# Zero products issued beside the weighted sums in the first grouped-query unit and the first neighbourhood head of each layer's attention

## The chip, the cores and the metric

The kernel runs on one core of a Trainium2 chip. The metric is the device time of one execution in microseconds (us). The time before is the median of three runs. A separate profiled execution gives the rows that are read below.

## What is computed

Two layers of a transformer block work on 1024 latent tokens and 256 context tokens of width 1024. Each layer has a token-mixing part with four parallel groups, and an MLP. Two of the four groups matter here: grouped-query attention (four query heads, two key heads of 64) and neighbourhood attention (four heads of 64, a window of 8 x 16 on a grid of 64 columns, with a learned bias). Cut to that:

```python
def attend(qi, kk, vv):
    s = jnp.einsum('bqkgd,bskd->bkgqs', qi, kk).astype(jnp.float32)
    p = jax.nn.softmax(s, axis=-1).astype(vv.dtype)
    return jnp.einsum('bkgqs,bskd->bqkgd', p, vv)
...
z = modulate(rms_norm(x, g_pre_mix), sh1, sc1) @ w_in
oa, oac = gqa_mixer(z, zc, ...)
ob, obc = s5_mixer(z, zc, ...)
on, onc = na_mixer(z, zc, ...)
od = fourier_mixer(z, w_fnet, b_fnet)
y = jnp.concatenate([oa, ob, on, od], axis=-1) @ w_out
x = x + g1 * rms_norm(y, g_post_mix)
h = modulate(rms_norm(x, g_pre_mlp), sh2, sc2)
x = x + g2 * rms_norm(sq_relu_mlp(h, w_mlp1, w_mlp2), g_post_mlp)
```

The context tokens go through the same weights in the first layer alone, where they are queries too.

## The kernel before

Tokens are cut into ten tiles of 128 (eight latent, two of context). A layer runs the input projection, then a phase that the function `attention` lays out, then the output projection and the MLP. Most products on TensorE are split into three (lines 161 to 163: high by high, low by high, high by low part), so that four-byte precision is kept.

The attention phase is a list of units that run one after the other. Six grouped-query units come first in layer 0 (two key heads, each with two blocks of four query tiles and one block of two context tiles) and four in layer 1, then four neighbourhood heads. A unit has two halves:

- The preparation, `gqa_prep` or `na_prep`. It transposes queries and keys (line 522), makes the scores once to find the largest of each row (products at lines 586 and 593, VectorE's maxima at 588 and 595; in a neighbourhood head 720, 729 and 747 with VectorE at 722, 730 and others), and writes the negative maximum as one more row of the queries. For a grouped-query unit the transposes of `ql` (line 522) carry it there. For a neighbourhood head it goes through a transpose (line 752), a copy to `nmt` and a DMA into the queries.
- The main half, `gqa_main` or `na_main`. For each key tile it makes scores already less the maximum (lines 653 or 778, two products that add up), ScalarE takes the exponential (654 or 782), and the weighted sums follow one key tile later (`pv`, line 622): products of 65 columns, of which the last is the sum of the weights. At the end VectorE divides (`divide`), and `finish` transposes the result (line 683).

The sums of a unit stand in one tile of two PSUM banks, `po`, of which there is one buffer. `sums` (line 613) opens both banks with a product of zeros: one row of 128 zeros by one row of as many zeros as the sums have columns (260 for a unit of four tiles, 130 for the context unit, 325 for a head with context queries). A unit's sums thus wait until the division of the unit before has read `po`. Scores have their own two buffers (`s1`), and the preparation has others.

The main half of a unit is woven with the preparation of the next one, and with the scan of the S5 group (lines 1291 to 1324) and the Fourier group (161 to 163 on `uh`, `csh`). The order of the instructions on each engine is set when the kernel is built: a scheduler walks through the program with its own estimate of durations and takes, among the instructions that are ready, the one of the best priority. On the chip every engine then takes its instructions strictly in that order. TensorE is one such queue, so a product that waits holds all that stand behind it.

Of the kernel before, what the change touches and what calls it, by code (L numbers as in the profile page):

```python
# [19 lines left out]
NT = 10  # L20
# [12 lines left out]
class K:  # L33
# [571 lines left out]
        self.transposes(q2, lambda i: ql[:, i // n, i % n, :], 2 * n)  # L605
        yield

    def sums(self, n):


        po = self.ps2(tag="pO")
        for b in range(2):
            self.nc.tensor.matmul(po[:, b * 512:b * 512 + n * 65], self.zero[:, :128], self.zero[:, :n * 65],
                                  start=True, stop=False)
        return po

    def pv(self, queue, vf, kt, po, parts, end=()):


        def whole():  # L620
            for (b, c), e in parts:
                self.nc.tensor.matmul(po[:, b * 512 + c * 65:b * 512 + c * 65 + 65], e, vf[:, kt, :],  # L622
                                      start=False, stop=(b, c) in end)
        queue.append((2, whole))
# [12 lines left out]
    def gqa_main(self, st, u, o):  # L637
        nc = self.nc
        q1, q2 = u["q"]
        k1, k2 = u["k"]  # L640
        vf = st["zg"][:, :, 384 + 65 * u["j"]:449 + 65 * u["j"]]
        w = u["n"] * 128
        kts = range(8, NT) if u["b"] == 2 else range(NT)
        po = self.sums(u["n"])
        queue = []
        for kt in kts:
            ks = slice(kt * 128, (kt + 1) * 128)
            e = st["pg"].tile([128, 1024], F32, tag="e", bufs=4, name="e")[:, :2 * w]
            for h in range(2):
                ps = self.ps1(tag="s1")[:, :w]  # L650
                hs = slice(h * w, (h + 1) * w)
                for kk, qq in ((k1, q1), (k2, q2)):
                    nc.tensor.matmul(ps, kk[:, ks], qq[:, hs], start=kk is k1, stop=kk is k2)
                nc.scalar.activation(e[:, hs], ps, AF.Exp)  # L654
            yield
            self.due(queue)
            self.pv(queue, vf, kt, po, [((h, t), e[:, h * w + t * 128:h * w + (t + 1) * 128])
                                        for h in range(2) for t in range(u["n"])],
                    [(h, u["n"] - 1) for h in range(2)] if kt == NT - 1 else ())
            yield  # L660
        self.due(queue, True)
        n = u["n"]
        on = st["fp"].tile([128, 4, 2, 64], F32, tag="on", bufs=2, name="on")
        self.divide(st, po, on[:, :n].rearrange("p t h d -> p h t d"), n)
        st["fin"] = self.finish(lambda t: on[:, t].rearrange("p h d -> p (h d)"), n, o, u["j"], u["t0"])
        yield
# [91 lines left out]
    def na_main(self, st, u, o):  # L758
        nc, s = self.nc, st["n"][u["h"] % 2]
        h, nq, bt = u["h"], u["nq"], s["bt"]  # L760
        k1, k2, q1, q2 = (s[n] for n in ("k1", "k2", "q1", "q2"))
        po = self.sums(nq // 256)
        queue = []
        for i, kt in enumerate((8, 0, 1, 2, 3, 4, 5, 6, 7, 9)):
            ks = slice(kt * 128, (kt + 1) * 128)
            ra, rb = (0, 16) if kt >= 8 else self.NA_ROWS_OF[kt]
            pieces = [(x * 64, y * 64) for x, y in ((ra, min(rb, 8)), (max(ra, 8), rb)) if x < y]

            r0 = ra - ra % 2
            e = st["pg"].tile([128, 1024], F32, tag="e", bufs=4, name="e")[:, :(rb - r0) * 64]  # L770
            if r0 < ra:
                nc.gpsimd.memset(e[:, 0:64], 0.0)
            f0 = (ra - 2 * kt + 6) if kt < 4 else 12 + (ra - 2 * kt + 3)
            for x, y in pieces:
                ps = self.ps1(tag="s1")[:, :y - x]
                ee = e[:, x - r0 * 64:y - r0 * 64]
                for kk, qq in ((k1, q1), (k2, q2)):
                    nc.tensor.matmul(ps, kk[:, ks], qq[:, x:y], start=kk is k1, stop=kk is k2)
                if kt < 8:
                    self.tt(ee, ps, bt[:, f0 + x // 64 - ra:f0 + y // 64 - ra, :].rearrange("p a b -> p (a b)"), OP.add)  # L780
                    ps = ee
                nc.scalar.activation(ee, ps, AF.Exp)
            yield
            self.due(queue)
            self.pv(queue, s["vf"], kt, po, [((t % 2, t // 2), e[:, t * 128 - r0 * 64:(t + 1) * 128 - r0 * 64])
                                             for t in range(r0 // 2, rb // 2)], [(0, 3), (1, 3)] if i == 9 else ())
            yield
            if i == 0 and nq > NLAT:

                ps = self.ps1(tag="s1").rearrange("p (b n) -> p b n", b=2)  # L790
                for c in range(2):
                    ks = slice(1024 + c * 128, 1152 + c * 128)
                    nc.tensor.matmul(ps[:, c, :], k1[:, ks], q1[:, 1024:1280], start=True, stop=False)
                    nc.tensor.matmul(ps[:, c, :], k2[:, ks], q2[:, 1024:1280], start=False, stop=True)
                e = st["pg"].tile([128, 1024], F32, tag="e", bufs=4, name="ec")[:, :512]
                nc.scalar.activation(e.rearrange("p (b n) -> p b n", b=2), ps, AF.Exp)
                yield
                self.due(queue)
                for c in range(2):
                    self.pv(queue, s["vf"], 8 + c, po, [((t, 4), e[:, c * 256 + t * 128:c * 256 + (t + 1) * 128])  # L800
                                                        for t in range(2)])
                yield
        self.due(queue, True)
        if h % 2 == 0:
            st["on"] = st["fp"].tile([128, NT, 2, 64], F32, tag="onn", bufs=1, name="onn")
        on = st["on"]
        n = nq // 256
        self.divide(st, po, on[:, :2 * n, h % 2].rearrange("p (c b) d -> p b c d", b=2), n)
        st["fin"] = iter(())
        if h % 2:  # L810
            st["fin"] = self.finish(lambda t: on[:, t].rearrange("p h d -> p (h d)"), 2 * n, o, 4 + h // 2, 0)
        yield
# [1036 lines left out]
```

## Time and profile before

| | us |
|---|---|
| median of three runs | 3044.02 |
| lowest and highest of the three | 3028.48 and 3049.46 |
| the profiled execution, its own time | 3037.68 |
| its span, first to last instruction | 3035.5 |
| TensorE busy in it | 2916.6 |

TensorE (PE) is busy in 96% of the span. PEld is its loading of weights, which lies beside its products. DVE is VectorE, ACT ScalarE, POOL GpSimd. [...] Times in rows are us from the start of the span, and "idle before <-releaser" is how long the engine stood still ahead of the instruction and whose result ended that.

### The profile page before, as it was taken

What the parts mean: (1) busy time and instruction counts of PE and PEld (TensorE: products, weight loads), DVE (VectorE), ACT (ScalarE), POOL (GpSimd) and SP (SyncE); (2) the same over time, 40 slices, a digit from 0 to 9 for tenths busy, and PEclk for the clock granted to TensorE, in tenths of its full rate; (3) what the DMA queues carried; (4) which work ended last, traced back from release to release, by engine and by line L of the source; (5) the groups of instructions that cost most, each with busy time, mean ns of one, the idle gap of its engine ahead of it and who ended that gap; (6) DMA issues with size and microseconds to landing.
All of it is one profiled execution on the core that took longest, in us unless ns stands there. A gap on an engine that the chain in (4) does not pass through costs nothing. (4 is left out here: it accounts for less than half of the span.)

```text
span 3035.5 us, 41960 instructions
## 1 busy us (share of the span) xinstructions
PE 2916.6 (96%) x16492; PEld 2538.7 (84%) x16492; DVE 1635.7 (54%) x2245; ACT 1078.5 (36%) x1850; POOL 912.6 (30%) x859
## 2 busy tenths in 40 slices
PE   6999999999999999999999899999999999999998
PEld 3798898888888889898988788888877888888887
DVE  3565565664776544754554676565754343344334
ACT  3544555453422222422222345365643212211222
POOL 1474223125421112611212555123234111111113
PEclk8999899999999999999999999999999999999999
DMA  7533425332543322432332534425343111111113
GB/s 267 187 115 116 93 79 140 113 138 97 184 141 132 129 84 84 160 118 98 111 117 99 169 110 133 92 73 154 106 160 111 56 42 56 42 56 42 56 42 111
DMA packets 233494, 334.87 MB, mean 110 GB/s; under 512 B 43120, under 2 KB 179408, under 8 KB 233296
## 3 DMA queue, kind: packets, MB, share of 16 engines
q1 hardware_dynamic: 233296, 332.18, 35.0%
q8 instruction: 130, 2.13, 0.3%
q14 instruction: 68, 0.56, 0.1%
HBM read 278.53 MB, written 53.54 MB: 109 GB/s over the span
## 5 line engine op out<-in xcount | busy, mean ns | idle before, releaser
L161 PE MATMUL ps<-mh,wh 128*128 128x320 f32 (+1 forms) x1536 | 518.9, 338 | 9.3 <-DVE y L155 6.1
L149 ACT ACTIVATE wh<-raw 128x1024 fp32r<-128x1024 f32 x234 | 243.1, 1057 | 795.3 <-PE ps L163 551.1
L163 PE MATMUL ps<-mh,wl 128*128 128x320 f32 (+1 forms) x1536 | 517.1, 337 | 0.9 <-DVE wl L152 0.9
L162 PE MATMUL ps<-ml,wh 128*128 128x320 f32 (+1 forms) x1536 | 517.6, 337 | 0.0
L161 PE MATMUL ps<-wh,hidh 128*128 128x512 f32 x1152 | 451.6, 392 | 2.1 <-DVE y L155 2.0
L163 PE MATMUL ps<-wh,hidl 128*128 128x512 f32 x1152 | 447.8, 390 | 2.7 <-POOL hidl L152 2.7
L162 PE MATMUL ps<-wl,hidh 128*128 128x512 f32 x1152 | 449.2, 390 | 0.0
L155 DVE TENSOR_TENSOR y<-ps,y 128x1024 f32<-128x1024 f32 (+1 forms) x253 | 306.6, 1218 | 260.5 <-PE ps L163 260.4
L152 POOL TENSOR_TENSOR hidl<-r,hidh 128x640 fp32r<-128x640 f32 (+1 forms) x128 | 190.5, 1489 | 679.6 <-DVE r L155 654.9
L152 DVE TENSOR_TENSOR wl<-raw,wh 128x1024 fp32r<-128x1024 f32 x188 | 286.4, 1533 | 176.0 <-ACT wh L149 167.5
L161 PEld LDWEIGHTS ps<-mh,wh 128*128 128x128 f32 x1536 | 290.0, 189 | 34.8 <-issue 7.3
L163 PEld LDWEIGHTS ps<-mh,wl 128*128 128x128 f32 x1536 | 289.9, 189 | 21.5 <-DVE wl L152 1.5
L162 PEld LDWEIGHTS ps<-ml,wh 128*128 128x128 f32 x1536 | 289.9, 189 | 20.8
L161 PEld LDWEIGHTS ps<-wh,hidh 128*128 128x128 f32 x1152 | 216.7, 188 | 53.2 <-issue 5.8
L152 POOL TENSOR_TENSOR wl<-raw,wh 128x1024 fp32r<-128x1024 f32 x48 | 117.4, 2447 | 467.3 <-ACT wh L149 467.1
L163 PEld LDWEIGHTS ps<-wh,hidl 128*128 128x128 f32 x1152 | 216.5, 188 | 48.9 <-POOL hidl L152 3.5
L162 PEld LDWEIGHTS ps<-wl,hidh 128*128 128x128 f32 x1152 | 216.7, 188 | 43.3
L155 DVE TENSOR_TENSOR r<-r 128x640 f32<-128x640 f32 (+1 forms) x128 | 98.9, 773 | 241.4 <-ACT hidh L1515 241.3
L1513 ACT ACTIVATE r<-ps 128x640 f32<-128x640 f32 (+1 forms) x128 | 82.3, 645 | 366.2 <-PE ps L163 360.4
L622 PEld LDWEIGHTS ps<-zg,e 128*128 128x128 f32 x1312 | 181.8, 195 | 15.0 <-ACT e L654 0.8
L622 PE MATMUL ps<-zg,e 128*128 128x65 f32 x1312 | 175.6, 270 | 0.4 <-ACT e L654 0.4
L294 DVE SCALAR_TENSOR_TENSOR acc<-raw,cst,acc 128x1024 f32<-128x1024 f32 x70 | 99.3, 1443 | 136.0 <-DMA raw<-in_w_ada_dram 136.0
(434 smaller groups left out, 5448.0 us busy)
## 6 DMA issues: line engine op xcount, KB each, us to landing
raw<-in_w_mlp_dram SPq DMA_DIRECT2D x192, 512.0 KB
raw<-in_w_ada_dram SPq DMA_DIRECT2D x96, 512.0 KB
raw<-in_w_in_dram SPq DMA_DIRECT2D x28, 512.0 KB
x<-x SPq DMA_DIRECT2D x26, 512.0 KB
x<-h SPq DMA_DIRECT2D x18, 512.0 KB
x<-in_x_dram SPq DMA_DIRECT2D x16, 512.0 KB
raw<-in_w_out_dram SPq DMA_DIRECT2D x16, 512.0 KB
bq<-in_na_bq_dram SPq DMA_DIRECT2D x8, 800.0 KB
```

The costliest lines, as they stand in the source:

```text
L149: self.nc.scalar.activation(out, in_, AF.Copy, scale=scale)
L152: (eng or self.nc.vector).tensor_tensor(out=out, in0=a, in1=b, op=OP.subtract)
L155: (eng or self.nc.vector).tensor_tensor(out=out, in0=a, in1=b, op=op)
L161: self.nc.tensor.matmul(ps, ah, bh, start=start and i == 0, stop=False)
L162: self.nc.tensor.matmul(ps, ah, bl, start=False, stop=False)
L163: self.nc.tensor.matmul(ps, al, bh, start=False, stop=stop and i == n - 1)
L294: nc.vector.scalar_tensor_tensor(acc[c], x, col, acc[c], op0=OP.mult, op1=OP.add)
L622: self.nc.tensor.matmul(po[:, b * 512 + c * 65:b * 512 + c * 65 + 65], e, vf[:, kt, :], start=False, stop=(b, c) in end)
L1513: nc.scalar.activation(r.rearrange("p (b n) -> p b n", b=nb), ps[:, :nb, :w], AF.Relu)
```

## The change

Four stages are marked as idle: the first grouped-query unit of each layer, and neighbourhood head 0 of each layer. In a marked stage three things differ.

First, bank 0 of `po` is opened 512 wide instead of 260 (or 325). Second, after the weighted sums of each key tile eight products of zeros are issued, 128 columns wide, into columns 384 to 512 of that bank, which the sums do not use. Each has one row of 128 zeros as its weights and one row of 128 zeros as its data, in bf16. They are issued at a priority lowered by 60, which gives the scheduler leave to place them later than their place in the program. Third, the flag that closes bank 0 moves from the last weighted sum to one more product of zeros, 512 wide, which stands ahead of the division.

There are ten key tiles in each marked stage, so 80 products of zeros in each, 320 in all, with four closing ones and four wider opening ones. No other instruction is added or taken away. Apart from these, the order of instructions differs only in the attention phases of the two layers.

```diff
-    def sums(self, n):
+    def sums(self, n, idle=False):
         po = self.ps2(tag="pO")
         for b in range(2):
-            self.nc.tensor.matmul(po[:, b * 512:b * 512 + n * 65], self.zero[:, :128], self.zero[:, :n * 65],
-                                  start=True, stop=False)
+            w = 512 if idle and not b else n * 65
+            self.nc.tensor.matmul(po[:, b * 512:b * 512 + w], self.zero[:, :128], self.zero[:, :w], start=True, stop=False)
         return po
+
+    def idle(self, po, n, end=False):
+        if end:
+            self.nc.tensor.matmul(po[:, 0:512], self.zero[:, :128], self.zero[:, :512], start=False, stop=True)
+            return
+        with self.tc.high_priority(offset=-60):
+            for _ in range(n):
+                self.nc.tensor.matmul(po[:, 384:512], self.zero[:, :128], self.zero[:, :128], start=False, stop=False)
...
+        idle = u is st["units"][0]
+        po = self.sums(u["n"], idle)
...
-                    [(h, u["n"] - 1) for h in range(2)] if kt == NT - 1 else ())
+                    [(h, u["n"] - 1) for h in range(idle, 2)] if kt == NT - 1 else ())
+            if idle:
+                self.idle(po, 8)
             yield
         self.due(queue, True)
+        if idle:
+            self.idle(po, 0, True)
...
-        po = self.sums(nq // 256)
+        po = self.sums(nq // 256, h == 0)
...
+            if h == 0:
+                self.idle(po, 8)
             yield
...
         self.due(queue, True)
+        if h == 0:
+            self.idle(po, 0, True)
```

In the changed kernel `sums` stands at line 614, the closing product at 621, the products of zeros at 625, the weighted sums at 632, the scores at 664 (before: 653) and 793 (778), the head's score maxima at 744 (729), the transposes of the result at 698 (683). Lines below 613 keep their numbers.

Where the products of zeros stand is the scheduler's choice. On TensorE, at the start of unit 0 of layer 0, the kernel before has these rows (`g0k` and `g0q` are the keys and queries of unit 0, `g1q` the queries of the next unit, `ql` the queries that carry the maximum):

```order
L653 MATMUL ps<-g0q_2780,g0k_2776 128x512 x2
L586 MATMUL ps<-g0k_2776,g0q_2780 128x512
L613 LDWEIGHTS zero
L613 MATMUL ps<-zero 128x260
...
L586 MATMUL ps<-g0k_2776,g0q_2780 128x512 x5
L593 MATMUL ps<-g0k_2776,g0q_2780 128x256 x8
L522 MATMUL ps<-identr,ql 128x128 x8
```

In the changed kernel the same place reads as follows, with the pair of L625 rows sixteen times:

```order
L664 MATMUL ps<-g0q_2780,g0k_2776 128x512 x2
L586 MATMUL ps<-g0k_2776,g0q_2780 128x512
L614 LDWEIGHTS zero
L614 MATMUL ps<-zero 128x512
...
L614 MATMUL ps<-zero 128x260
L625 LDWEIGHTS zero
L625 MATMUL ps<-zero 128x128
...
L586 MATMUL ps<-g0k_2776,g0q_2780 128x512 x5
L593 MATMUL ps<-g0k_2776,g0q_2780 128x256 x8
L522 MATMUL ps<-identr,ql 128x128 x8
```

Sixteen products of zeros, those of two key tiles, stand right behind the opening of the sums, ahead of the five remaining products whose maxima VectorE waits for, and none stands behind those.

On TensorE at the end of unit 0 of layer 0, the kernel before has these rows (`g1q` are the queries of unit 1, `khl` the keys of the next key head, `on` the result of unit 0):

```order
L622 MATMUL ps<-zg,e 128x65 x4
L653 MATMUL ps<-g1q_3290,g0k_2776 128x512
L653 MATMUL ps<-g1q_3291,g0k_2777 128x512
...
L522 MATMUL ps<-identr,ql 128x128 x4
L522 MATMUL ps<-identr,khl 128x128 x4
L653 MATMUL ps<-g1q_3290,g0k_2776 128x512
L653 MATMUL ps<-g1q_3291,g0k_2777 128x512
L613 LDWEIGHTS zero
L613 MATMUL ps<-zero 128x260
```

The changed kernel has these, with the pair of L625 rows two times at the first place and six times at the second:

```order
L625 LDWEIGHTS zero
L625 MATMUL ps<-zero 128x128
...
L664 MATMUL ps<-g1q_3290,g0k_2776 128x512
L664 MATMUL ps<-g1q_3291,g0k_2777 128x512
L625 LDWEIGHTS zero
L625 MATMUL ps<-zero 128x128
...
L632 MATMUL ps<-zg,e 128x65 x6
L522 MATMUL ps<-identr,khl 128x128 x4
L632 MATMUL ps<-zg,e 128x65 x5
L522 MATMUL ps<-identr,khl 128x128 x2
L632 MATMUL ps<-zg,e 128x65 x4
L621 MATMUL ps<-zero 128x512
```

Weighted sums of unit 0 and products of zeros now stand between the first scores of unit 1 and the transposes of the keys, where before the scores of unit 1 ended the stage.

On TensorE in neighbourhood head 0 of layer 0 the kernel before has these rows (`n0` is head 0, `n1` head 1 in preparation, `nvf` the values):

```order
L729 MATMUL ps<-n1k_5228,n1q_5232 128x512
L778 MATMUL ps<-n0q_4891,n0k_4887 128x512
L778 MATMUL ps<-n0q_4892,n0k_4888 128x512
L778 MATMUL ps<-n0q_4891,n0k_4887 128x256
L778 MATMUL ps<-n0q_4892,n0k_4888 128x256
L622 MATMUL ps<-nvf_4893,e 128x65 x5
L729 MATMUL ps<-n1k_5228,n1q_5232 128x512 x2
L778 MATMUL ps<-n0q_4891,n0k_4887 128x192
```

The changed kernel has these, where the pairs of L625 rows stand three, two, eight and three times, in this order:

```order
L793 MATMUL ps<-n0q_4972,n0k_4968 128x512
L793 MATMUL ps<-n0q_4973,n0k_4969 128x512
L625 LDWEIGHTS zero
L625 MATMUL ps<-zero 128x128
...
L744 MATMUL ps<-n1k_5309,n1q_5313 128x512
L625 MATMUL ps<-zero 128x128
...
L632 MATMUL ps<-nvf_4974,e 128x65 x3
L625 MATMUL ps<-zero 128x128
...
L632 MATMUL ps<-nvf_4974,e 128x65 x2
L793 MATMUL ps<-n0q_4972,n0k_4968 128x256
L793 MATMUL ps<-n0q_4973,n0k_4969 128x256
L632 MATMUL ps<-nvf_4974,e 128x65 x2
L625 MATMUL ps<-zero 128x128
...
```

Here the products of zeros are scattered ahead of and behind the products of L744 whose maxima VectorE takes.

## Rows read from the trace of the kernel before

**Rows 1.** The page: span, busy time, granted clock in 40 slices

```profile
span 3035.5 us, 41960 instructions
...
PE 2916.6 (96%) x16492; PEld 2538.7 (84%) x16492; DVE 1635.7 (54%) x2245; ACT 1078.5 (36%) x1850; POOL 912.6 (30%) x859
...
PEclk8999899999999999999999999999999999999999
```

**Rows 2.** Busy time of each engine in stretches of the attention phases

```profile
core 0: us, PE busy (x) PEld busy (x) DVE busy (x) ACT busy (x) POOL busy (x), PEclk, DMA share, GB/s
...
315.07:328.73 13.66, 12.12 (x43) 9.72 (x44) 6.47 (x12) 5.89 (x9) 2.16 (x3) 0.50 0.81 153
328.73:362.86 34.13, 34.13 (x251) 31.71 (x250) 23.62 (x48) 21.71 (x43) 11.33 (x19) 1.00 0.33 85
...
366.27:376.51 10.24, 10.24 (x48) 8.99 (x47) 0.82 (x1) 6.14 (x13) 0.59 (x2) 0.50 0.02 8
...
516.46:536.94 20.48, 20.01 (x82) 18.74 (x83) 12.99 (x31) 9.13 (x22) 8.93 (x11) 0.50 0.28 91
...
550.59:554.01 3.42, 3.42 (x16) 3.11 (x15) 2.39 (x7) 1.07 (x2) 0.00 (x0) 0.50 1.02 220
...
1932.99:1939.82 6.83, 5.73 (x19) 4.03 (x18) 3.18 (x5) 5.44 (x9) 1.94 (x2) 0.50 1.22 137
1939.82:1977.37 37.55, 37.18 (x277) 34.91 (x277) 26.71 (x50) 22.23 (x44) 15.21 (x22) 1.00 0.43 116
2096.83:2110.48 13.65, 9.56 (x38) 8.35 (x38) 7.17 (x17) 2.57 (x6) 0.24 (x2) 0.50 0.83 222
2110.48:2137.00 26.52, 26.22 (x216) 24.62 (x215) 20.64 (x46) 17.87 (x38) 11.45 (x17) 1.00 0.41 131
```

**Rows 3.** All zero products of line 613: ns of one (min/median/max), forms

```profile
L613 PEld LDWEIGHTS <-zero x36: 90/93/112, 308.8 to 2196.7; 1*128 1x128 bf16 x36
L613 PE MATMUL ps<-zero x36: 215/279/418, 308.8 to 2196.8; 1*128 1x260 bf16 x24, 1*128 1x325 bf16 x8, 1*128 1x130 bf16 x4
```

**Rows 4.** Timeline of PE: a 130-column pair of zero products; start, us

```profile
495.47 0.28 PE L613 MATMUL ps<-zero 1*128 1x130 bf16 x2
```

**Rows 5.** Timeline of PE, start of unit 0 of layer 0

```profile
308.22 0.39 PE L653 MATMUL ps<-g0q,g0k 128*128 128x512 f32 x1
308.45 0.40 PE L586 MATMUL ps<-g0k,g0q 128*128 128x512 f32 x1
308.78 0.39 PE L613 MATMUL ps<-zero 1*128 1x260 bf16 x2
309.10 1.03 PE L586 MATMUL ps<-g0k,g0q 128*128 128x512 f32 x2
```

**Rows 6.** Timeline of DVE in the same place

```profile
308.89 4.01 DVE L588 TENSOR_REDUCE nm<-ps 128x1 f32<-128x512 f32 x6 [0.35 <-PE ps L586]
312.81 2.66 DVE L595 TENSOR_REDUCE nm<-ps 128x2 f32<-128x512 f32 x4
```

**Rows 7.** Timeline of PE, start of head 0 of layer 1

```profile
2099.84 0.61 PE L613 MATMUL ps<-zero 1*128 1x260 bf16 x2 [4.07 <-DVE on L155]
2100.38 0.27 PE L752 MATMUL ps<-identr,nmr 128*16 128x128 f32 x1
...
2107.41 1.19 PE L778 MATMUL ps<-n0q,n0k 128*128 128x512 f32 x2 [1.08 <-DMA n0q<-nmt]
```

**Rows 8.** Timeline of PE in head 0 of layer 0

```profile
515.23 0.50 PE L729 MATMUL ps<-n1k,n1q 128*128 128x512 f32 x1 [0.78 <-DVE mx L730]
516.58 0.80 PE L729 MATMUL ps<-n1k,n1q 128*128 128x512 f32 x1 [0.84 <-DVE mx L730]
```

**Rows 9.** Timeline of PE, end of unit 0 of layer 0

```profile
365.86 0.89 PE L653 MATMUL ps<-g1q,g0k 128*128 128x512 f32 x2 [1.48 <-ACT e L654]
366.68 0.61 PE L613 MATMUL ps<-zero 1*128 1x260 bf16 x2
```

**Rows 10.** Timeline of PE, head 0 to head 1 of layer 0

```profile
549.55 0.39 PE L161 MATMUL ps<-uh,fwh 128*128 128x258 f32 x1 [2.27 <-DVE gl L152]
```

More of the change, by code (lines that the diff above doesn't have):

```diff
@@ L643, in gqa_main @@
         kts = range(8, NT) if u["b"] == 2 else range(NT)
-        po = self.sums(u["n"])
+        idle = u is st["units"][0]
+        po = self.sums(u["n"], idle)
         queue = []
@@ L785, in na_main @@
             self.pv(queue, s["vf"], kt, po, [((t % 2, t // 2), e[:, t * 128 - r0 * 64:(t + 1) * 128 - r0 * 64])
-                                             for t in range(r0 // 2, rb // 2)], [(0, 3), (1, 3)] if i == 9 else ())
+                                             for t in range(r0 // 2, rb // 2)], [(b, 3) for b in range(h == 0, 2)] if i == 9 else ())
+            if h == 0:
+                self.idle(po, 8)
             yield
```

## The prediction

> **What bounds the kernel now.** I read the page first. TensorE is busy for 2916.6 us of a span of 3035.5 us, and its granted clock is a little under full in a few slices only [rows 1]. So the kernel is bound by TensorE almost everywhere, and a change that gives TensorE more to do has to earn its time back somewhere. The place to look for that is the clock. [...] Three things are to be seen there. At the start of unit 0 of layer 0 the low stretch lasts 13.66 us, but TensorE is busy for only 12.12 of it and VectorE is what it waits for. At the end of that unit a low stretch of 10.24 us is filled with TensorE's work to the last: 48 products and nothing else that counts. In head 0 of layer 0 a low stretch lasts 20.48 us with 20.01 busy. Layer 1 has two more, 6.83 and 13.65 us, with gaps in them, and between head 0 and head 1 of layer 0 there is one of 3.42 us. Between these stretches TensorE is at 1.00 and full: 34.13 of 34.13 us in unit 0 of layer 0, 37.18 of 37.55 in that of layer 1, 26.22 of 26.52 in head 0 of layer 1 [rows 2]. A product of zeros that stands there delays all that follows.
>
> **What one product of zeros costs.** The kernel already has such products, of 260, 325 and 130 columns. Their weight load takes 0.09 us [rows 3]. The pair of 130 columns lasts 0.28 us, of which the last product is 0.215 (the shortest) [rows 3, 4]. So the two start 0.065 us apart, and I take that for 128 columns; the load lies under the product before. A pair of 260 columns lasts 0.39 us with 0.27 to 0.28 for one, so 0.12 apart [rows 3, 5]. At the low clock the pair lasts 0.61 us with 0.418 for the longest one, so 0.19 apart [rows 3, 9]; a product of 128 columns is then about 0.10. A change between two kinds of product costs a little too: the 512-wide products before the pair start 0.23 us apart, but the pair starts 0.33 after the last of them, and the next product 0.32 after the pair, where twice 0.12 would do [rows 5]. That is 0.10 in and 0.08 out. The products of zeros stand in 66 groups, and where a group stands between score products and weighted sums TensorE changes kind anyway. I take 0.10 a group; the ends are 0 and 0.18.
>
> [...]
>
> **The sum of what is added.**
> A, start of unit 0 of layer 0: all first 16 products and 252 more opening columns stand ahead of products whose maxima VectorE takes. VectorE works without a stop there, from 308.89 for 4.01 us and on for 2.66 [rows 6], and the transposes of `ql` wait for it. So a delay of TensorE counts in full: 16 x 0.065 + 252 x 0.12/260 = 1.2 us.
> B, the full stretches: 64 products in 19 groups in the rest of unit 0 of layer 0, 69 in 19 in unit 0 of layer 1, 64 in 12 in head 0 of layer 1: 197 x 0.065 + 50 x 0.10 = 17.8 us. TensorE has no gap there that could hide them [rows 2].
> C, start of unit 0 of layer 1, eleven products as in A: 11 x 0.065 + 0.12 = 0.8 us.
> D, start of head 0 of layer 1: sixteen products stand behind the opening, which waits 4.07 us for the division, and ahead of the transpose at 2100.38, from which a chain leads through the DMA of `nmt` to the scores at 2107.41 [rows 7]. At the low clock: 16 x 0.10 + 252 x 0.19/260 = 1.8 us, all on the chain.
> E, four closing products of 512 columns, 0.23 us each [rows 5]. Two lie in full stretches, two ahead of waits: I count half, 0.5 us.
> F, head 0 of layer 0, 80 products in 16 groups: 80 x 0.065 + 16 x 0.10 + 0.1 for the wider opening = 6.9 us, less what lies in TensorE's waits for VectorE, 0.78 and 0.84 us [rows 8]: 5.3 us.
> Together 1.2 + 17.8 + 0.8 + 1.8 + 0.5 + 5.3 = 27.4 us.
>
> **What the clock gives back.** A low stretch can go if the waits of TensorE ahead of it are filled.
> G, end of unit 0 of layer 0. Before it TensorE waits 1.48 us for an exponential [rows 9]. In the changed kernel eight products of zeros and sixteen weighted sums stand between the score pairs there. I expect the stretch to go: 10.24 us at half clock become 5.1, a gain of 5.1 us. VectorE has 0.82 us to do in it, so it is not late next [rows 2].
> H, head 0 of layer 0. Ahead of the stretch are the waits of 0.78 and 0.84 us [rows 8], and products of zeros now stand among those that wait. TensorE's 20.01 us would become 10.0, but VectorE has 12.99 us to do in the same stretch [rows 2] and is late next. The most is 7.5 us; I take 6.5, since TensorE and VectorE do not meet without gaps.
> I, head 0 to head 1 of layer 0: TensorE waits 2.27 us [rows 10], then 3.42 us go at the low clock [rows 2]. I take half of 3.42 and 0.3 of the wait, 2.0 us.
> The stretch at 315.07 stays: its sixteen products come before VectorE's 6.7 us of maxima, and none is left for the gap behind them. So does that at 2096.83, since its products stand behind the wait for the division.
> Together 13.6 us, with ends 0 and, as the rivals show, about 25.
>
> **The sum.** 27.4 - 13.6 = 13.8 us more. On the profiled execution's own 3037.68 us that is 3051.5; on the median of 3044.02, which stands 6.3 us higher, it is 3057.8. I forecast 3054, between them. The three runs of before lie 21 us apart, so I tell 1% (about 30 us, the least that a measurement of this kernel can tell from no change) from no change and nothing smaller.
>
> **The rivals.**
> First, no stretch goes (slower). The clock falls after the wait in G and H all the same, since the products of zeros stand behind products that themselves wait: TensorE takes its queue in order, and a wait ahead of them leaves them as late as the rest. For this speaks that most of the products stand in full stretches and few in the gaps. It costs the 27.4 us, and at 0.18 a group another 66 x 0.08 = 5.3: 3065 to 3070 on the profiled time, up to 3077 on the median. It decides from the point at which less than half of the 13.6 us comes back; beyond 30 us it is over 1% slower.
> Second, more stretches go (no slower, or a little faster). The stretches at 315.07, 1932.99 and 2096.83 shorten as well: 12.12 us of TensorE's work would become 6.1, with 6.47 for VectorE beside it, so up to 6 us; a half of 5.73, so 2.5; and 3 of 13.65 us [rows 2], 11.5 together. If kinds also change at no cost (6.6 less), the sum is 13.8 - 11.5 - 6.6 = -4.3 us: 3033 on the profiled time, 3040 on the median. Against it speaks where the products stand.
> Third, the loads are not hidden. If each load of the zeros waits for the product before it, a product of zeros costs 0.09 + 0.065 = 0.155 us, 320 of them 49.6 instead of 20.8, and the sum is 13.8 + 28.8 = 42.6 us, 3080 to 3087. The pair of 130 columns, 0.065 apart with a load of 0.09 [rows 3, 4], speaks against it.
> [...]
>
> **How the numbers follow.** The forecast (11 to 17 us more, some 3040 to 3065 with the spread of runs) has a chance of 0.55, the first rival 0.20, the second 0.22, the third 0.03. Slower by over 1% are the third and a fifth of the first: 0.07. Faster by over 1% needs 30 us off, and if all six low stretches (68 us together [rows 2]) ran at the full clock, half of them less 27.4 would leave 7; a tenth of the second is left for it: 0.02. Within 1% is the rest, 0.91. The range goes from 3032, the low end of the second, to 3072, past most of the first; about 2 in 10 lie outside.
>
> **What would show it.** The profile after should have TensorE busy for some 20 us more at the lines of the zeros, no low stretch at the end of unit 0 and in head 0 of layer 0, and the low stretch at the start of unit 0 as before. It is wrong if the products of zeros start 0.09 us or more apart, if the low stretches of G and H are still there, or if the one at 315.07 is gone.

## The result and the profile after

The changed kernel takes 3089.3 us (median of four executions, 3087.7 to 3093.22), the kernel before 3046.74 beside it. The ratio is 1.0153, with an interval of 1.0118 to 1.0188: slower by 1.5%. I had forecast 3054 us, within 1%, with a range up to 3072. The prediction was wrong in size, and the clock moved the other way from the one I gave it.

The page of the changed kernel, in the lines that answer to [rows 1] (PEclk is TensorE's granted clock as a share of full speed; its mean over the span is 0.970 here and 0.974 before):

```profile
span 3087.8 us, 42616 instructions
...
PE 2968.8 (96%) x16816; PEld 2570.9 (83%) x16816; DVE 1631.8 (53%) x2245; ACT 1077.9 (35%) x1850; POOL 907.9 (29%) x859
...
PEclk8999998999999999999999999997999999999999
```

TensorE has 324 products more and is busy 52 us longer, at the same share of a longer span. One digit of the clock has fallen to 7: that is the slice of head 0 of layer 1. The table of stretches answers to [rows 2] (same columns; the first three are the start and the end of unit 0 of layer 0, then head 0 of layer 0, the start of unit 0 of layer 1, and head 0 of layer 1 with what follows):

```profile
311.57:321.81 10.24, 8.31 (x29) 6.01 (x30) 6.41 (x12) 5.30 (x8) 2.09 (x2) 0.50 1.01 174
321.81:363.95 42.14, 42.14 (x303) 34.49 (x303) 26.57 (x52) 23.91 (x47) 14.77 (x23) 1.00 0.33 85
363.95:374.19 10.24, 10.24 (x83) 9.22 (x83) 2.41 (x4) 6.24 (x13) 0.53 (x2) 1.00 0.13 38
512.95:550.50 37.55, 37.55 (x172) 32.45 (x172) 17.14 (x41) 11.63 (x26) 8.73 (x15) 0.50 0.15 47
1949.96:1956.79 6.83, 5.86 (x21) 4.01 (x20) 3.17 (x5) 5.59 (x9) 2.55 (x3) 0.50 1.11 223
2120.63:2168.42 47.79, 41.40 (x187) 35.94 (x188) 22.19 (x48) 14.39 (x31) 8.74 (x15) 0.50 0.36 98
2168.42:2191.36 22.94, 22.94 (x185) 18.99 (x184) 12.65 (x26) 11.35 (x22) 6.41 (x6) 1.00 0.47 133
```

The reader is to see two things. The low stretch at the end of unit 0, 10.24 us in [rows 2], is gone, as forecast: the place runs at 1.00. But in head 0 of layer 0 the low stretch has grown from 20.48 to 37.55 us, and TensorE is busy for all of it; in head 0 of layer 1 from 13.65 to 47.79 us. TensorE's timeline in that last stretch shows what it did while the clock stayed down:

```profile
2140.58 1.80 PE L632 MATMUL ps<-nvf,e 128*128 128x65 f32 x8
2142.14 1.20 PE L793 MATMUL ps<-n0q,n0k 128*128 128x512 f32 x2
2143.14 1.80 PE L632 MATMUL ps<-nvf,e 128*128 128x65 f32 x8
2144.87 0.60 PE L625 MATMUL ps<-zero 1*128 1x128 bf16 x4
2145.40 0.80 PE L744 MATMUL ps<-n1k,n1q 128*128 128x512 f32 x1
2146.13 0.60 PE L625 MATMUL ps<-zero 1*128 1x128 bf16 x4
2146.66 0.80 PE L744 MATMUL ps<-n1k,n1q 128*128 128x512 f32 x1
```

No row carries a wait. From 2135 us to the end of the stretch TensorE went from product to product with no gap in its list, real ones and products of zeros by turns, at a clock of 0.50 for 33 us. In the kernel before the clock was back at 1.00 3 us after the scores of that head began at 2107.41 [rows 2, 7]. A full low stretch alone does not convict the products of zeros, though: one of the experiments below has a low stretch of 30.72 us that is just as full, with three of them in it.

**A split that needs no single stretch.** Where a low stretch lies and how long it lasts differs from one execution to the next. Each execution has a span and a mean granted clock, though. In the traces of before and of the change the clock is 1.00 or 0.50 at any time, 20 low stretches in each. Span x (1 - clock) is then half of the time at 0.50, the most that the low clock can have cost; I call it the cost of the low clock. The rest, span x clock, I call the time at full clock. This is an account and not a measurement of what a full clock would give: where TensorE waits within a low stretch, less would come back. The means over executions (± is the standard error) are steady enough to compare, and the sections below use them; differences are taken before rounding. The kernel before stands at 2958.2 ± 0.4 and 82.0 ± 1.1 us (73 executions), the change at 2991.8 ± 1.0 and 98.9 ± 2.5 us (10 executions, of the result and of the repeat below). One slow execution of the kernel before, of 3077.67 us, is left out. So of the 50.6 us between the spans (3040.2 and 3090.8), 33.7 lie in the time at full clock, and 16.9 are the clock's.

### The profile page after: what moved, and what is told of

Read it like the earlier page. It is cut to its first block, busy times and chain, and to the rows that moved or that the text cites. A ratio compares the mean times of both kernels' runs of the same rounds, so it can differ in the third digit from the quotient of the medians.

```text
span 3087.8 us, 42616 instructions
## 1 busy us (share of the span) xinstructions
PE 2968.8 (96%) x16816; PEld 2570.9 (83%) x16816; DVE 1631.8 (53%) x2245; ACT 1077.9 (35%) x1850; POOL 907.9 (29%) x859
```

## The experiments

Theory A says that products of one row occupy TensorE but do not bring its clock back, and that they also keep real products from doing so. Its rivals are that the products simply take their time and the order of the real ones makes the rest (B), that the closing product costs it (C), and that the changed order lowers the clock (D).

**All 128 rows.** The products take a tile of zeros of 128 rows:

```diff
-                self.nc.tensor.matmul(po[:, 384:512], self.zero[:, :128], self.zero[:, :128], start=False, stop=False)
+                self.nc.tensor.matmul(po[:, 384:512], self.zf, self.zf, start=False, stop=False)
```

`zf` is a tile of zeros, 128 by 128, that one more memset fills at the start.

> Edit: each of the 320 products takes all 128 rows of a tile of zeros as weights and as data, where the change takes one row; columns, type and number are the same. Theory A (clock): products of one row fill TensorE's queue but do not bring its clock back, so the low stretches in the two heads 0 grew from 20.48 to 37.55 us and from 13.65 to 47.79 us. Then with 128 rows both should be about as long as before (20 us or less, 14 us or less), head 0 of layer 1 takes under 55 us instead of 67.84, and the time is some 3055 to 3065 us. Theory B (queue and order): TensorE is slower because real products stand in another order and the products take its time. Then rows make no difference: both stretches stay within 5 us of 37.55 and 47.79, and the time stays within 10 us of 3089.

Measured: 3055.98 us (ratio 1.0047, 1.0022 to 1.0073). At full clock 2987.5 ± 1.1, for the low clock 67.9 ± 3.2 us: less than before the change. The time is where theory A put it, head 0 of layer 0 has no low stretch in the profile, and head 0 of layer 1 took 54.62 us. Its low stretch, of 20.48 us, is longer than the 14 that theory A allowed. The scheduler also placed some real products otherwise, so this run alone does not shut out theory B.

**32 rows**, with the order of the change:

```diff
-                self.nc.tensor.matmul(po[:, 384:512], self.zero[:, :128], self.zero[:, :128], start=False, stop=False)
+                self.nc.tensor.matmul(po[:, 384:512], self.zf[:32], self.zf[:32], start=False, stop=False)
```

> Edit: each of the 320 products takes 32 rows of zeros as weights and as data, where the change takes one; the order of every engine is that of the change, row for row. Theory A (clock, by rows): 32 rows do a quarter of what 128 do, so the low stretches in the two heads 0 shorten by something, or hardly at all; the time lies between 3065 and 3090 us. Theory B (queue and order): as the change, 3089 us, with the low stretches of 37.55 and 47.79 us within 5 us.

Measured: 3082.78 us (1.0128, 1.009 to 1.0167); low clock 85.5 ± 5.9 us over four executions, too few to decide. The low stretches in the two heads 0 lasted 23.89 and 44.37 us in the profile. The kernel was run again, below.

**Heads alone, and units alone.** The first pair of lines is the edit for the heads alone, the others for the units alone:

```diff
-        idle = u is st["units"][0]
+        idle = False
...
-        po = self.sums(nq // 256, h == 0)
+        po = self.sums(nq // 256, False)
...
-            if h == 0:
+            if False:
```

> Edit: the products, the wider opening and the closing product in the two heads 0 alone, none in the two first grouped-query units. Theory A (clock): heads 0 of both layers carry 38 of the 52 us by which the profiled execution became longer, so some 3080 us, with long low stretches in both heads (over 30 us). Theory B (queue and order): half of the products leave, so about half of the loss goes: some 3068 us.

> Edit: the products, the wider opening and the closing product in the two first grouped-query units alone, none in the heads. Theory A (clock): the units carry some 17 us of direct cost and give back 7 us behind them by the low stretch at the end of unit 0 of layer 0, so some 3055 us, and the low stretches of the heads are as before (about 20 and 14 us). Theory B (queue and order): half of the loss, some 3068 us.

Measured: heads alone 3083.88 us (1.012, 1.0056 to 1.0184), 2966.1 ± 2.1 at full clock and 112.5 ± 11.0 for the low clock, over four executions that lie 45 us apart. Units alone 3057.31 us (1.0059, 1.0032 to 1.0086), 2976.1 ± 0.9 and 82.0 ± 3.1. The two halves seem to cost different things: in the units the products cost TensorE's time and no clock that shows, in the heads little time and much clock, with low stretches of 54.61 and 44.37 us in the profile. Units alone fit theory A's 3055 and not theory B's 3068, which lies above the interval (3051 to 3067 us). Heads alone decide nothing by their time: the interval, 3058 to 3097 us, holds A's 3080 and B's 3068.

**64 rows**, in the order of the first kernel with 128 rows:

```diff
+                self.nc.tensor.matmul(po[:, 384:512], self.zf[:64], self.zf[:64], start=False, stop=False)
```

> Edit: each of the 320 products takes 64 rows of zeros. The order of every product on TensorE is that of the kernel with 128 rows, which differs in places from that of the change. Theory A (clock, by rows): 64 rows lie between 32 (3083 us) and 128 (3056 us); the low stretch in head 0 of layer 1 is longer than the 20.48 us of 128 rows, and the time is 3060 to 3082 us. Theory B' (the other order alone made the kernel with 128 rows faster): as 128 rows, 3056 us within 5, with low stretches like there.

Measured: 3077.96 us (1.01, 1.0067 to 1.0133). The time lies between, as theory A said, but for another reason than the one given: the low clock costs 74.5 ± 4.8 us, not clearly more than with 128 rows, and head 0 of layer 1 had a low stretch of 20.48 us like there. What is longer is the time at full clock, 2997.2 ± 1.1 against 2987.5. The price of changing rows, below, explains that.

**One product for each key tile:**

```diff
             if i % every == every - 1:
-                for _ in range(n):
+                for _ in range(1):
                     next(back, None)
...
         with self.tc.high_priority(offset=-60):
-            for _ in range(n):
+            for _ in range(1):
```

> Edit: one product of zeros (one row, as in the change) after each key tile instead of eight, 40 instead of 320; the wider opening and the closing products stay. Theory A (clock): 40 products are too few to hold the clock down for long; the low stretches in the heads 0 are close to those of before (some 20 and 14 us), and the time is 3043 to 3058 us. Theory C (the closing product, or the order around it, costs the time): the loss stays, 3075 us or more.

Measured: 3072.8 us (1.0084, 1.0061 to 1.0107), 2963.7 ± 1.4 at full clock and 105.3 ± 3.2 for the low clock. Neither theory's figure was met, but this run cannot be held against either, for the edit does more than its text says. Its first place is not the products but `weave`, which sets how many steps the preparation of the next unit goes on at each step of the main half: one now, where the attention phases ask for three. So the real products stand in quite another order, and nothing follows from this run about 40 products or about the closing product. The other kernels so far, but for the one with 32 rows, differ from the change in their order as well. So the same order had to be run with and without the products, below.

**A version to beat both.** 128 rows in layer 0 alone (both edits), and in head 0 of layer 0 alone (the second, with `idle = False` in the units):

```diff
-        idle = u is st["units"][0]
+        idle = u is st["units"][0] and st["l"] == 0
...
-            if h == 0:
+            if h == st["l"] == 0:
```

> Edit: the products with 128 rows, in layer 0 alone; layer 1 is as before. A version that may beat both. Theory A: in layer 0 the 128 rows keep the clock at full from unit 0 to head 3 (its head 0 took 48.5 us with them, 53.6 before, unit 1 39.5 instead of 44.0, unit 0 60.3 instead of 57.9), so some 8 us less than before: 3033 us. If the gain was chance of that run: 3041 to 3050 us.

> Edit: the products with 128 rows in neighbourhood head 0 of layer 0 alone; all else as before. Theory A: the low stretch of 20.48 us in that head goes, 5 to 7 us less than before: some 3035 us. Rival: the clock falls in that head all the same, and the products cost their 7 us: 3047 us.

Measured: 3052.36 us (1.004, 1.0019 to 1.006) and 3048.83 us (1.0017, 0.9995 to 1.004). Neither is faster than before. The first lies above both of its expectations, the second at its rival's 3047. The low clock costs 77.4 ± 3.3 and 81.0 ± 2.2 us, not clearly less than the 82.0 of before. In both profiled runs head 0 of layer 0 came out shorter (48.44 and 50.59 us against 53.59). But head 0 of layer 1, which has no product of zeros in these two kernels, took 55.29 and 59.71 us at a mean clock of 0.67 and 0.66. So a long low stretch came there without any product of zeros, and a single profile proves little about it.

**The order alone.** The order of the change is set with all products, and then 307 of the 320 are taken out of the program, with their weight loads:

```diff
+                if i.name in drop and free(i):
+                    gone.add(i.name)
+                    if isinstance(last, mybir.InstLdweights) and free(last):
+                        gone.add(last.name)
...
+            if gone:
+                b.instructions = [i for i in b.instructions if i.name not in gone]
```

> Edit: every engine's instructions stand in the order of the change, but 307 of the 320 products of zeros are taken out after the order is set (13 carry a semaphore and stay); the opening and closing products stay. Time is split as span x granted clock (what is left at full clock: 2958 us before, 2993 with the change) and span x (1 - granted clock) (what the low clock costs: 82 us before, 95 with the change). Theory A (the one-row products themselves hold the clock down): without them the low clock costs some 82 us as before, the rest some 2966 us, the span 3048 us. Theory D (the changed order of the real products brings the low clock, and the products of zeros do little against it): the low clock costs 95 to 110 us, the span is 3060 to 3075 us.

**The same order with 128 rows**, made from the kernel with 32 rows, the 320 products widened after the order is set:

```diff
+    full = lambda p: copy.replace(p, ap=((128, 128), (1, 128)), bass_ap=None) if p.memref.startswith("zf") else p
...
+                        new[m] = copy.replace(new[m], ins=tuple(map(full, new[m].ins)), tile_size=(128, 128))
```

> Edit: the order of the change, instruction for instruction, with the 320 products widened from one row to all 128 after the order is set. Theory A (rows): the low clock costs some 68 us as in the first kernel with 128 rows, the rest stays at about 2990 us, the span is some 3058 us. Theory B' (that kernel was faster by its other order): the low clock costs 90 to 100 us as in the change, the span is some 3085 us.

**The change again, and 32 rows again**, with no edit, beside these two:

> Edit: none, the change itself once more beside the others, since four executions are few for the split. All theories: span 3083 to 3092 us, some 2993 at full clock and 92 to 98 for the low clock. If the second is under 88 us, the first four executions were chance.

> Edit: none against the kernel with 32 rows, repeated beside the others. Theory A (rows): the low clock costs more than with 128 rows in the same order and less than with one, 75 to 90 us; the rest is some 2995 us. Without an effect of rows: as the change, 92 to 98 us.

Measured, the last four in one and the same order of instructions (the repeats put together with their first runs; us):

| products of zeros | executions | span | at full clock | cost of the low clock |
|---|---|---|---|---|
| kernel before, its own order, none | 73 | 3040.2 ± 1.0 | 2958.2 ± 0.4 | 82.0 ± 1.1 |
| order of the change, 13 left | 12 | 3058.0 ± 2.6 | 2971.8 ± 1.3 | 86.2 ± 2.5 |
| 320, one row (the change) | 10 | 3090.8 ± 2.2 | 2991.8 ± 1.0 | 98.9 ± 2.5 |
| 320, 32 rows | 10 | 3082.6 ± 2.9 | 2994.4 ± 1.2 | 88.2 ± 3.2 |
| 320, 128 rows | 10 | 3056.1 ± 2.1 | 2982.1 ± 1.0 | 74.0 ± 2.5 |

Run by run, the medians were 3058.43 (1.0064, 1.004 to 1.0088) for the order alone, 3057.35 (1.0059, 1.0032 to 1.0085) for 128 rows, 3094.89 (1.0181, 1.0145 to 1.0217) for the change, and 3086.47 (1.0152, 1.0114 to 1.019) for 32 rows. This table settles, for the given order, that the rows matter. From one row to 128 the low clock costs 24.9 us less (standard error 3.5), and the rows of weights and data are all that differs, but for one memset at the start; theory B, by which rows make no difference, is out. With 128 rows it costs 12.2 us less (3.5) than with next to no products: here such products do what filling a gap was expected to do. From the order alone to the change it costs 12.8 us more (3.5), and the products are all that differs. With 32 rows it costs 10.7 us less than with one (4.1) and about what it costs with none, 88.2 against 86.2.

Theory D is out as the whole cause: the order alone adds 4.1 us of low clock (2.7), which may be nothing, or half of the 16.9. Theory B' is out: with 128 rows the order makes no difference to the span that shows (3056.1 here, 3055.3 ± 2.7 in the other order). Theory C was not tested by itself. The opening and closing products stand in all four of these kernels, so what they cost is in the 17.8 us by which the order alone is above before.

How far theory A's second half holds, that products of one row also keep real products from bringing the clock back, stays open. Low stretches in the heads 0 of layers 0 and 1, first of the order alone and then of the change's repeat:

```profile
504.38:535.10 30.72, 30.72 (x130) 28.42 (x129) 17.39 (x41) 11.68 (x26) 9.59 (x15) 0.50 0.24 72
2108.64:2129.12 20.48, 14.47 (x57) 12.64 (x58) 11.88 (x26) 6.85 (x14) 0.24 (x2) 0.50 0.63 175
...
509.69:557.48 47.79, 47.40 (x209) 40.17 (x210) 20.79 (x47) 14.38 (x32) 8.73 (x15) 0.50 0.27 73
2137.85:2185.64 47.79, 43.92 (x198) 38.36 (x199) 20.12 (x43) 13.95 (x30) 8.72 (x15) 0.50 0.34 97
```

The order alone already has longer low stretches there than before (20.48 and 13.65 us). It lost others, at the end of unit 0 and behind head 0 of layer 0, so its mean clock in the profile is 0.974 as before. Of the products in these rows 3 and 1 are of zeros in the order alone, 45 and 48 in the change and 52 and 48 in its repeat. That leaves 127 and 56 real products at the low clock in the order alone, 127 and 139 in the change, 157 and 150 in the repeat. In layer 0 the first profile of the change thus has a longer low stretch with no more real work in it; in layer 1 more real work ran at the low clock. A part of the 12.8 us is simply the products' own time at the low clock:

```profile
2124.14 1.91 PE L625 MATMUL ps<-zero 1*128 1x128 bf16 x16
```

Sixteen last 1.91 us there and the longest of them 0.309, so they start 0.107 us apart, and the 93 of the change's profile take 10 us. Half of that, 5 us by this estimate, counts as the low clock's cost.

The stages of the two heads 0, from their opening to the next one, in the profiled runs (columns as in [rows 2]; head 0 of layer 0 first, then of layer 1). The kernel before:

```profile
500.38:553.97 53.59, 48.75 (x292) 44.14 (x291) 33.95 (x68) 23.61 (x50) 15.62 (x18) 0.78 0.59 153
...
2099.84:2143.39 43.55, 41.42 (x284) 37.27 (x285) 31.20 (x63) 23.98 (x51) 17.00 (x21) 0.88 0.58 163
```

The change:

```profile
500.76:568.36 67.60, 64.43 (x384) 55.14 (x383) 34.30 (x70) 25.48 (x54) 16.11 (x19) 0.72 0.44 118
...
2123.52:2191.36 67.84, 64.34 (x370) 54.93 (x370) 32.00 (x67) 25.10 (x52) 15.14 (x21) 0.67 0.40 111
```

Its order alone:

```profile
495.38:552.18 56.80, 54.89 (x307) 49.26 (x307) 34.36 (x70) 25.42 (x54) 16.96 (x19) 0.73 0.51 141
...
2111.63:2160.11 48.48, 45.45 (x293) 40.43 (x294) 31.77 (x67) 24.70 (x52) 15.09 (x21) 0.82 0.50 147
```

Its order with 128 rows:

```profile
497.53:545.93 48.40, 45.05 (x384) 40.06 (x383) 34.35 (x70) 25.49 (x54) 17.03 (x19) 1.00 0.60 165
...
2106.40:2157.67 51.27, 50.05 (x369) 44.51 (x370) 31.81 (x67) 24.91 (x52) 15.06 (x21) 0.83 0.49 142
```

VectorE's and ScalarE's busy times hardly differ among the three kernels of one order. What differs is the clock: 0.72 and 0.67 with one row, 1.00 and 0.83 with 128 rows, in the same order with the same count of products on TensorE (384, and 370 or 369 recorded). In layer 0 the order alone is nearly as low as the change (0.73). These are single profiles; the table above is the evidence.

## Why the prediction was wrong

**What the clock gives back** is the step that failed. I wrote that a low stretch can go if the waits ahead of it are filled, and counted 13.6 us for G, H and I. That was my estimate from the waits that [rows 8 to 10] show ahead of three stretches; no run shows it for products of one row. Against the kernel before, the low clock costs 16.9 us more. That is 30.5 of the 36.8 us by which the sum was short (50.6 us between the spans instead of 13.8). H failed outright: the stretch of 20.48 us, which I expected at half, lasted 37.55 us in the change and 47.79 in the repeat's profile. I also wrote that the stretch at 2096.83 stays, and it grew from 13.65 to 47.79 us. I had asked only whether TensorE's queue would be occupied. My own rows spoke against that: at the end of unit 0 TensorE was busy for 10.24 of 10.24 us at a clock of 0.50, and in head 0 of layer 0 for 20.01 of 20.48 [rows 2]. The runs show that what occupies it counts: in one order the low clock costs 98.9 us with products of one row, 86.2 with next to none and 74.0 with 128 rows.

**G and I held, but not for their reason.** The stretch at the end of unit 0 is gone in the change, but it is gone in the order alone too: the next unit takes 39.42 us at a clock of 1.00 there, 39.49 in the change and 44.04 at 0.89 before. The three profiled kernels that leave the first units without products (before, heads alone, head 0 of layer 0 alone) all have a low stretch of 10.24 us there; the other eleven, with 1, 32, 64 or 128 rows or with 13 products left, have none. So it goes with the rearranged weighted sums and transposes, not with the products. The stretch of 3.42 us behind head 0 of layer 0 is likewise absent in the change, in its repeat and in the order alone.

```profile
366.06:405.48 39.42, 39.42 (x294) 36.98 (x293) 24.63 (x48) 22.43 (x46) 4.95 (x10) 1.00 0.19 55
```

That row is of the order alone, from the opening of unit 1 to that of the next.

**The sum of what is added** was mis-sized in two terms that partly cancel. I counted 27.4 us, nearly all of it for the products. From the order alone to the change the time at full clock grows by 20.0 us for 307 products, so that is less: I take it that part of them lies in waits, as F allowed for one stage only, but that was not measured. The changed order of real products I put at nothing without a reason, and the opening and closing products at 1.0 us. The order alone, which still has these and 13 products of zeros, stands 13.7 us above before at full clock. Together 33.7 instead of 27.4.

By the profiles, about half of the 13.7 lies where no product of zeros stands. The order differs outside the attention phases as well, other than the section on the change says: in the output projection of layer 0 and the first half of its MLP TensorE takes its products in another sequence too. That part of the kernel before and of the order alone, up to the first product of `hidh`:

```profile
646.80:801.10 154.30, 152.18 (x752) 130.04 (x753) 74.96 (x61) 55.09 (x75) 74.86 (x61) 0.97 0.44 147
...
643.00:804.40 161.40, 152.82 (x753) 129.30 (x754) 77.80 (x62) 54.68 (x75) 76.92 (x61) 0.97 0.42 142
...
PE ps L324 <- POOL h L155: 4.8, 4, 1.9
```

TensorE has the same work and waits more, 8.6 us instead of 2.1. The last row (us in total, times, longest) is the largest of these waits in the order alone, transposes that wait for GpSimd; before has none. At full clock the part is 5.3 to 7.8 us longer than before in the profiles of the order alone, the change, its repeat and 128 rows. Another place is head 2 of layer 1, with no product of zeros in it: 31.3 us in the order alone and 23.2 before, both at a clock of 1.00; of these 8.1 us 5.4 come back by the output projection.

**The cost of one product** was close: 0.065 us forecast. A group of seven in the change starts at 340.56 and the score behind it at 341.05:

```profile
340.30 0.33 PE L632 MATMUL ps<-zg,e 128*128 128x65 f32 x2
340.56 0.56 PE L625 MATMUL ps<-zero 1*128 1x128 bf16 x7
341.05 0.74 PE L664 MATMUL ps<-g0q,g0k 128*128 128x512 f32 x2
341.72 0.22 PE L625 MATMUL ps<-zero 1*128 1x128 bf16 x1
341.87 2.00 PE L632 MATMUL ps<-zg,e 128*128 128x65 f32 x16
```

Seven last 0.56 us and the last of them 0.214, so they start (0.56 - 0.214)/6 = 0.058 us apart. The third rival, loads in series, is out by the same rows and this one:

```profile
L625 PEld LDWEIGHTS <-zero x320: 90/93/147, 306.1 to 2185.3; 1*128 1x128 bf16 x160
```

A load takes 0.09 us and the products start 0.058 apart, where the third rival has 0.155, so a load lies here beside the products before it.

**The change of kind** was mis-sized and misnamed. I took 0.10 a group, half of the 0.18, as the price of going between types. The same place in the same order with 128 rows:

```profile
342.12 0.33 PE L632 MATMUL ps<-zg,e 128*128 128x65 f32 x2
342.29 0.55 PE L625 MATMUL ps<-zf 128*128 128x128 bf16 x7
342.65 0.71 PE L664 MATMUL ps<-g0q,g0k 128*128 128x512 f32 x2
343.21 0.23 PE L625 MATMUL ps<-zf 128*128 128x128 bf16 x1
343.28 1.28 PE L632 MATMUL ps<-zg,e 128*128 128x65 f32 x10
```

The types are the same, but the group starts 0.17 us after the two weighted sums instead of 0.26, and the score follows after 0.36 instead of 0.49. So it is the number of rows that costs, some 0.1 us going in and as much coming out. It is paid at both ends of a group, not at one. Of the 69 groups 51 stand at full clock and without a wait in both profiles. From the product ahead of such a group to the one behind it the change takes 0.195 us more (median), 9.5 us over all 51; the time at full clock falls by 9.7 us from one row to 128.

**The rivals.** The first, no stretch goes, came nearest, with 3077 at its top. It let the clock stay as it was, and the clock became worse. I gave no case to that. The second, more stretches go, did not happen. The chance of 0.07 for slower by over 1% was too small because it was built on a clock that could only improve.

## What to carry to other kernels

Before products are added to keep TensorE's clock up, ask what they do beside filling the queue. A TensorE without a gap was at a clock of 0.50 for 33 us here, and for 30.72 us with hardly a product of zeros. In one order of instructions 128 rows cost TensorE 9.7 us less than one row, and the low clock 24.9 us less. Even so, products that were put into an engine that is full for most of the time cost here about what they gave back. With 128 rows the kernel is still 16 us slower than before: the order that the scheduler makes around them costs 13.7 us at full clock and perhaps 4.1 of low clock, the products take 10.3 and give 12.2 back. Split executions into span x clock and span x (1 - clock) before explaining a single low stretch; the same kernel's stretches differ by 10 us from run to run (37.55 and 47.79 us in head 0 of layer 0 of the change). To price instructions that are added, run the same order without them.

## What the runs showed that I had not expected

Between products of one row and of 128 rows TensorE loses some 0.1 us each way, at full clock (0.26 against 0.17 us going in and 0.49 against 0.36 to the score behind, above). The type is bf16 in both, between products of f32, so it is not the change of type. With 32 rows a group in the same order takes what it takes with one (the median difference of 50 groups at full clock and without a wait is 0.00 us). In the profile with 64 rows, too, the score behind a group of seven follows 0.49 us after the group's start:

```profile
342.85 0.56 PE L625 MATMUL ps<-zf 64*128 64x128 bf16 x7
343.34 0.73 PE L664 MATMUL ps<-g0q,g0k 128*128 128x512 f32 x2
```

And its time at full clock (2997.2 us) lies above that of 128 rows in the same order (2987.5). Products of 128 rows of zeros lowered the cost of the low clock from 86.2 to 74.0 us in one order, so zeros as data did not prevent it; other data were not run. Nor was it tried whether the rows of the weights or those of the data matter.
